# Five gather buffers, and a float32 activation in the fronts of a two-layer decoder step

## The chip, the core and the metric

The kernel runs on one core of a Trainium2 chip: TensorE (PE, with its weight loads as PEld), VectorE (DVE), ScalarE (ACT), GpSimd (POOL) and SyncE (SP) work side by side, each through its own instructions in a fixed order, and 16 DMA engines move data. The metric is the time of one execution in microseconds of the device; lower is better.

## The reference, cut to what matters

512 prompt tokens (four tiles of 128, numbered 0 to 3) and 8 sample tokens (tile 4) pass through two layers. Layer 0 is a gated MLP, layer 1 attention with shared keys and values; each is followed by the same expert block, which for each token picks 128 of 16384 experts:

```
q = (h @ w_q).reshape(T, 8, 2, 128)
s = einsum('thcd,hcnd->thcn', q, keys)        # 8 heads, 2 halves, 128 keys
sv, si = top_k(s, 16)                          # then the 16 best of the 256 sums per head
g = softmax(top_s)
u, vv = u_tab[eidx], v_tab[eidx]               # rows of 1024 numbers, 128 of each per token
act = gelu(einsum('thkd,td->thk', u, h))
out = einsum('thk,thkd->td', g * act, vv)
```

All numbers are float32.

## The kernel before, in words

**Two ways through the expert block.** In each layer two of the four tiles are done densely and two by gathering (`DT`: dense are tiles 0 and 1 in layer 0, tiles 2 and 3 in layer 1).

- *Gathered tiles* (`peer_tile`): for each of the 128 chosen experts GpSimd gathers one row of `peer_u` per token (`gather`, an indirect DMA of 512 KB into a tile of pool `gb`, tag `g`), and DVE multiplies it with `h_g` and sums it into a column of `act`. After 16 of them ScalarE applies the gelu, and 16 rows of `peer_v` are gathered and added to `x` by DVE. That makes 2 tiles x 256 = 512 gathers in each layer, 1024 in all, each with one DVE instruction over 128x1024 numbers. The pool has three buffers. A gather can be issued when the buffer that it takes has been read by DVE.
- *Dense tiles* (`dense_peer`): all 16384 experts are computed for 256 tokens, in four quarters of 32 blocks of 128 experts. `acts(q)` multiplies blocks of `peer_ut` (tile `ub`) with the activation, `gates(q)` builds the gates of the chosen experts by one-hot matrices and multiplies them in (`W`, L531), and the loop at the end multiplies `W` with blocks of `peer_v` (tile `vb`) into four PSUM banks `y`. The third and fourth quarters' `acts`, half of the second's, and the whole fourth quarter of `y`, are split products.

**Split products.** A float32 number is written as a sum of two float32r numbers, high and low; TensorE takes three float32r passes (high x high, high x low, low x high) in place of one float32 product. For a weight block `split` makes the high part on ScalarE (`wh`, L206) and the low part on DVE (`wl`, L208, one instruction of 128x1024). For the activation `norm_T` and `to_T` make the high part on ScalarE and the low part on DVE (`hTl`, L179 and L200).

**Fronts.** Before its expert block each layer has two groups of tiles (`GROUPS`): layer 0 first tile 2 alone, then tiles 0, 1, 3, 4; layer 1 first tile 0, then tiles 2, 3, 1, 4. `stage` counts these four fronts from 0. A front is the gated MLP or the attention, then `peer_front`: normalise, queries by `peer_wq` (16 weight blocks), scores against the keys, and the ranking on DVE (`topk_rank`, `topk_pick`). In the first front of a layer, which has one tile (and in layer 1 the sample's keys), products are float32. In the second, with up to 392 columns, `split_T` returns a float32r pair and `dense` splits each weight block; only `w_out` and `w_q` are float32 there. In the first quarter of `dense_peer` the pair is added up again into two float32 tiles `hF` (L538).

**What sets the order.** The program is traced once, and a scheduler with a model of the engines lays each engine's instructions in a fixed order. A list of anchors (`tick`) ties the n-th gather product of a layer to the n-th anchor, so that the gathers spread over the work beside them; this decides the place in the order and is no wait on the chip. Each engine then runs its order strictly: a DVE instruction that waits for a gather holds up all that stands behind it. Gathers of a layer start when the first front has chosen its tile's experts (`ix`, L671) and must be done before the next layer's front of those tiles.

**Buffers that the change touches.** Tag `h` (`HB[0]`: four of 128x1024 in layer 0, three in layer 1), tag `zT` (three), the activation `hT` in the permanent pool, `row4` for the sample tokens' rows of keys and queries, and a tile `cand` each for 8 heads and 1.

Of the kernel before, what the change touches and what calls it, by code (L numbers as in the profile page):

```python
# [18 lines left out]
D = 1024  # L19
S = 512  # L20
NB = 8
# [14 lines left out]
def body(ctx: ExitStack, tc: tile.TileContext, a):  # L36
# [4 lines left out]
    gb = ctx.enter_context(tc.tile_pool(name="gb", bufs=3))  # L41
# [35 lines left out]
    HB, NW = [4], [264]  # L77
# [105 lines left out]
    def split_T(name, both=False):  # L183

        if stage[0] == 2 or 1 and not stage[0]:
            return wa.tile([128, 8, 128], F32, name=name, tag="h", bufs=HB[0])
        pool, tag, n = (per, "hT", 392) if stage[0] else (wa, "hA", 256)
        if [0, 0, 0, 0][stage[0]] and not both:
            return pool.tile([128, 8, n], F32, name=name, tag=tag + "h", bufs=1)
        return [pool.tile([128, 8, n], FR, name=name + k, tag=tag + k, bufs=1) for k in "hl"]  # L190
# [20 lines left out]
    def dense(w, nk, rhs, n, consume, f0=0, f1=None, steps=None):  # L211

        f1 = w.shape[0] if f1 is None else f1
        for f in range(f0, f1):
            ps = pm.tile([128, 512], F32, name="ps_d", tag="mm")
            for c0 in range(0, nk, 8):
                wt = wp.tile([128, 8, 128], F32, name="wt", tag="wt")
                SY.dma_start(wt, w[f, :, c0:c0 + 8, :])
                if isinstance(rhs, list):
                    wh, wl = split(wt, [1, 2, 1, 2][stage[0]])  # L220
                    for c in range(8):
                        PE.matmul(ps[:, :n], wh[:, c, :], rhs[0][:, c, :n], start=c == 0, stop=False)  # L222
                        PE.matmul(ps[:, :n], wh[:, c, :], rhs[1][:, c, :n], start=False, stop=False)  # L223
                    for c in range(8):
                        PE.matmul(ps[:, :n], wl[:, c, :], rhs[0][:, c, :n], start=False, stop=c == 7)
                else:
                    for c in range(8):
                        z = PE.matmul(ps[:, :n], wt[:, c, :], rhs[:, c0 + c, :n], start=c0 + c == 0,  # L228
                                      stop=c0 + c == nk - 1)
                    tick(z, [6, 6, 6, 5][stage[0]])  # L230
            consume(f - f0, ps)
            step([4, 6, 4, 5][stage[0]] if steps is None else steps)

    def to_tok(n, tiles, func, tok):
        hold = {}

        def consume(ft, ps):
            q, i = divmod(ft, ZF)
            if i == 0:
                hold[0] = wa.tile([128, ZF, NW[0]], F32, name="zT", tag="zT", bufs=3)  # L240
# [23 lines left out]
    def gmlp(tiles, n, ph):  # L264
# [54 lines left out]
        def u_out(ft, ps):  # L319
            if ft % ZF == 0:  # L320
                hold[0] = wa.tile([128, ZF, NW[0]], F32, name="uT", tag="zT", bufs=3)
# [36 lines left out]
    def topk_rank(s, p, nh, state, h0):  # L358
# [14 lines left out]
        cand = wk.tile([128, nh, 88], F32, name="cand", tag=f"cand{nh}", bufs=1)[:p]  # L373
# [92 lines left out]
    def dense_peer(layer, dpa, open_rest, open_odd, smp):  # L466
        hT = dd["hT"]
        NQ, QI, NV = 4, 32, 4
# [4 lines left out]
        def acts(q):  # L473

            W[q] = (odd if q % 2 else dpa).tile([128, QI, 256], F32, name="W", tag="W", bufs=1)
            for il in range(QI):
# [3 lines left out]
                if (il * 5) % 32 < [[0, 16, 32, 32], [0, 16, 32, 32]][layer][q]:  # L480
                    uh, ul = split(u, [2, 3][layer] if q else [0, 1][layer])
                    for c in range(8):
                        PE.matmul(ps, uh[:, c, :], hT[0][:, c, :256], start=c == 0, stop=False)  # L483
                        PE.matmul(ps, uh[:, c, :], hT[1][:, c, :256], start=False, stop=False)  # L484
                    for c in range(8):
                        PE.matmul(ps, ul[:, c, :], hT[0][:, c, :256], start=False, stop=c == 7)  # L486
                else:
                    for c in range(8):
                        for k in range(2):
                            z = PE.matmul(ps[:, k * 128:(k + 1) * 128], u[:, c, :], hF[k][:, c, :], start=c == k == 0,  # L490
                                          stop=c == 7, skip_group_check=True)
                    tick(z, [2, 3][layer] if q else [0, 1][layer])
# [3 lines left out]
        def gates(q):  # L496
# [4 lines left out]
            for t0 in range(0, 256, 32):  # L501
# [32 lines left out]

        hF = [dpa.tile([128, 8, 128], F32, name=f"hF{k}", tag=['vb', 'vb'][k], bufs=3 if ['vb', 'vb'][k] == "vb" else 1)
              for k in range(2)]
        for k in range(2):
            V.tensor_tensor(hF[k], *[z.bitcast(F32)[:, :, k * 128:(k + 1) * 128] for z in hT], op=OP.add)  # L538
# [50 lines left out]
    def peer_front(tiles, n, layer, ph):  # L589
        if any(t == 4 or t not in DT[layer] for t in tiles):  # L590
            gbc = bcast_row(a["f_norm_g"][layer], D, f"g_f{layer}")
        hT = dd["hT"] = split_T("hT", True)
# [23 lines left out]
        if 4 in tiles:  # L616
            qz = [wa.tile([128, 8, 72], F32, name=f"qz{c}", tag="zT", bufs=3) for c in range(2)]
# [82 lines left out]
    def gather(table, ix, k, pool=None, tag="sg", nb=1):  # L700
        t = gb.tile([128, D], F32, name="gath", tag="g") if pool is None else \
            pool.tile([128, D], F32, name="gaths", tag=tag, bufs=nb)
# [64 lines left out]
    def run_layer(layer, setup):  # L767
# [11 lines left out]
        HB[0], NW[0] = 4 - layer, GROUPS[layer][1][1]  # L779
# [58 lines left out]
    def setup1(ph):  # L838
# [182 lines left out]
        def attn(tiles, n):  # L1021
# [6 lines left out]
            if first:  # L1028
                hT = per.tile([128, 8, 392], F32, name="hT", tag="hTh")
# [3 lines left out]
                row4 = per.tile([128, 2, D], F32, name="row4", tag="hTl")[:NB]  # L1033
                smp["v"] = ks.tile([128, D], F32, name="v_smp", tag="hs", bufs=1)[:NB]
                smp["kT"] = ph.tile([128, 8, NB], F32, name="kTs")
            else:
                hT = split_T("hT")
# [12 lines left out]
            def row(t, k):  # L1050
                return wa.tile([128, D], F32, name="kq_tok", tag="h", bufs=HB[0]) if t < 4 else row4[:, k]

            kt = {t: row(t, 0) for t in kqv}
# [9 lines left out]
            qt = {t: row(t, 1) for t in kqv}  # L1063
# [19 lines left out]
            oT = split_T("oT")  # L1083
# [120 lines left out]
```

## Time and profile before

| | |
|---|---|
| median of three runs | 3507.37 us (3499.5 to 3507.73) |
| the profiled execution | 3478.04 us, span 3476.3 us, granted TensorE clock 0.93 on the mean |
| busy: PE, PEld, DVE, ACT, POOL | 88%, 70%, 73%, 41%, 37% of the span |
| chain that ended last | PE 37%, DMA 27%, DVE 15%, issue 14%, POOL 6% |
| of it the gathers' DMAs | 15% `peer_v`, 9% `peer_u` |
| moved | 976.76 MB, on the mean 281 GB/s |

A busy share is the mean over stages with different limits, so it is read stage by stage. A wait is the idle time of an engine before an instruction and what ended it. In the chain, "issue" is time in which an engine waited for nothing that the profile shows.

### The profile page before, as it was taken

How to read it: one execution, taken by the hardware profiler on the slowest of the kernel's cores; microseconds unless marked ns; L12 is line 12 of the kernel's file. 1: busy time of each engine (PE TensorE's matmuls, PEld its weight loads, DVE VectorE, ACT ScalarE, POOL GpSimd, SP SyncE). 2: the span in 40 equal slices, each digit the busy share in tenths (PEclk: the TensorE clock that was granted, in tenths of full speed). 3: DMA queues.
4: the chain of work that ended last, by engine and by line, in shares of the span. 5: the costliest groups of instructions: out<-in, count | busy, mean ns of one | idle time of the engine just before them, and what ended most of it. 6: DMA issues, size and time to landing. Idle time of an engine off the chain costs nothing.

```text
span 3476.3 us, 53629 instructions
## 1 busy us (share of the span) xinstructions
PE 3063.4 (88%) x19776; PEld 2450.6 (70%) x19776; DVE 2545.1 (73%) x5191; ACT 1421.2 (41%) x3180; POOL 1289.9 (37%) x1061
## 2 busy tenths in 40 slices
PE   7988948779999999999888888646899999999998
PEld 7887538779757857757878643546899658758656
DVE  1478569888666777668657677779888666777778
ACT  2343022125565485664444344322236334343433
POOL 0034442334344344434320433442334444334343
PEclk9998979889999999999999988769899999999999
DMA  7677875778888989889985777775788889889888
GB/s 257 226 253 253 276 241 189 254 277 284 299 310 308 332 304 320 318 292 327 332 287 179 281 256 248 261 235 176 270 301 311 313 300 321 318 291 341 304 278 316
DMA packets 271576, 976.76 MB, mean 281 GB/s; under 512 B 30938, under 2 KB 31770, under 8 KB 271306
## 3 DMA queue, kind: packets, MB, share of 16 engines
q0 software_dynamic: 152064, 553.72, 46.5%
q1 hardware_dynamic: 119250, 419.62, 34.5%
q8 instruction: 155, 2.54, 0.3%
q14 instruction: 107, 0.88, 0.1%
HBM read 966.76 MB, written 6.46 MB: 280 GB/s over the span
## 4 chain that ended last, share of the span: by engine, by line
PE 37%; DMA 27%; DVE 15%; issue 14%; POOL 6%; ACT 1%; POOLq 0%; DVEq 0%; SPq 0%; ACTq 0%
DMA gath<-peer_v,ix 15%; PE y L573 10%; DMA gath<-peer_u,ix 9%; POOL gath L703 6%; PE ps_d L228 4%; DVE gath L712 3%; PE ps_g L528 3%; DVE x L719 3%; PE ps_a L486 3%; PE ps_a L490 3%; PE ps_a L483 3%; PE ps_a L484 3%; PE y L570 1%; DVE wl L208 1%; PE y L571 1%
## 5 line engine op out<-in xcount | busy, mean ns | idle before, releaser
L703 POOL DMA_INDIRECT gath<-peer_u,ix x512 | 634.2, 1239 | 1212.4 <-DVE gath L712 631.1
L703 POOL DMA_INDIRECT gath<-peer_v,ix x512 | 612.6, 1197 | 910.4 <-DVE x L719 531.4
L712 DVE SCALAR_TENSOR_TENSOR gath<-gath,h_g 128x1024 f32<-128x1024 f32 x512 | 622.9, 1222 | 298.0 <-DMA gath<-peer_u,ix 295.9
L719 DVE SCALAR_TENSOR_TENSOR x<-gath,act,x 128x1024 f32<-128x1024 f32 x512 | 656.2, 1282 | 246.1 <-DMA gath<-peer_v,ix 241.5
L573 PE MATMUL y<-vb,W 128*128 128x512 f32 x1536 | 718.6, 611 | 5.2 <-DVE W L531 5.2
L521 ACT ACTIVATE ohj<-iota,selJ 128x128 f16<-128x128 f32 x1408 | 423.8, 388 | 352.0 <-PE ps_g L528 351.7
L573 PEld LDWEIGHTS y<-vb,W 128*128 128x128 f32 x1536 | 285.4, 196 | 292.6 <-issue 287.2
L490 PE MATMUL ps_a<-hF,ub 128*128 128x128 f32 x3072 | 362.5, 281 | 50.9 <-DVE hF L538 50.3
L490 PEld LDWEIGHTS ps_a<-hF,ub 128*128 128x128 f32 x3072 | 358.6, 198 | 52.7 <-DVE hF L538 50.7
L528 PEld LDWEIGHTS <-ohj 128*128 128x128 f16 x4096 | 257.6, 130 | 94.1 <-issue 86.5
L483 PE MATMUL ps_a<-hTh,wh 128*128 128x256 f32 x1280 | 320.3, 288 | 0.0
L484 PE MATMUL ps_a<-hTl,wh 128*128 128x256 f32 x1280 | 312.4, 282 | 0.0
L528 PE MATMUL ps_g<-gi,ohj 128*128 128x32 f16 x4096 | 269.9, 233 | 11.6 <-DVE gaths L731 8.1
L206 ACT ACTIVATE wh<-ub 128x1024 fp32r<-128x1024 f32 x160 | 169.6, 1060 | 255.0 <-PE ps_a L484 205.0
L483 PEld LDWEIGHTS ps_a<-hTh,wh 128*128 128x128 f32 x1280 | 243.1, 190 | 3.4 <-issue 2.9
L484 PEld LDWEIGHTS ps_a<-hTl,wh 128*128 128x128 f32 x1280 | 242.7, 190 | 3.4 <-issue 3.4
L222 PE MATMUL ps_d<-hTh,wh 128*128 128x392 f32 (+1 forms) x640 | 230.7, 362 | 12.2 <-ACT qT L637 5.3
L223 PE MATMUL ps_d<-hTl,wh 128*128 128x392 f32 (+1 forms) x640 | 226.4, 355 | 3.5 <-DVE hTl L200 3.2
L208 DVE TENSOR_TENSOR wl<-ub,wh 128x1024 fp32r<-128x1024 f32 x160 | 194.9, 1222 | 43.2 <-ACT wh L206 37.8
L531 DVE TENSOR_TENSOR W<-ps_g,W 128x512 f32<-128x512 f32 x128 | 156.7, 1225 | 83.0 <-PE ps_g L528 82.5
L493 ACT ACTIVATE W<-ps_a 128x256 f32<-128x256 f32 x256 | 94.7, 374 | 275.1 <-PE ps_a L490 217.8
L206 ACT ACTIVATE wh<-wt 128x1024 fp32r<-128x1024 f32 x88 | 93.3, 1061 | 242.5 <-PE ps_d L223 168.3
(313 smaller groups left out, 4662.0 us busy)
## 6 DMA issues: line engine op xcount, KB each, us to landing
ub<-peer_ut SPq DMA_DIRECT2D x256, 512.0 KB, 5.2
vb<-peer_v SPq DMA_DIRECT2D x256, 512.0 KB, 5.3
wt<-w_in SPq DMA_DIRECT2D x64, 512.0 KB, 4.5
wt<-peer_wq SPq DMA_DIRECT2D x64, 512.0 KB, 4.3
wt<-w_out SPq DMA_DIRECT2D x32, 512.0 KB, 4.5
gath<-peer_u,ix POOLq DMA_INDIRECT x512, 6.1
gath<-peer_v,ix POOLq DMA_INDIRECT x512, 6.2
wt<-w_k SPq DMA_DIRECT2D x16, 512.0 KB, 5.6
```

The lines of the kernel that those rows point to most:

```text
L206: SC.activation(wh, w, AF.Copy)
L208: tick(V.tensor_tensor(wl, w, wh.bitcast(F32), op=OP.subtract), k)
L222: PE.matmul(ps[:, :n], wh[:, c, :], rhs[0][:, c, :n], start=c == 0, stop=False)
L483: PE.matmul(ps, uh[:, c, :], hT[0][:, c, :256], start=c == 0, stop=False)
L484: PE.matmul(ps, uh[:, c, :], hT[1][:, c, :256], start=False, stop=False)
L490: z = PE.matmul(ps[:, k * 128:(k + 1) * 128], u[:, c, :], hF[k][:, c, :], start=c == k == 0, stop=c == 7, skip_group_check=True)
L521: SC.activation(oh[:, :, k], iota128, AF.Abs, scale=-1.0, bias=selJ[:, t2 + k:t2 + k + 1])
L528: PE.matmul(ps[:, t - t1, :], oh[:, :, k], gi[:, c, :, t - t0], start=c == 0, stop=c == 1)
L573: PE.matmul(y[t][hf], w[:, ts], v[:, hs], start=i == 0, stop=i == 127)
L703: GP.indirect_dma_start(out=t, out_offset=None, in_=table, in_offset=bass.IndirectOffsetOnAxis(ap=ix[:, k:k + 1], axis=0))
L712: z = V.scalar_tensor_tensor(u, u, 1.0, h, op0=OP.mult, op1=OP.mult, accum_out=act[:, k:k + 1])
L719: z = V.scalar_tensor_tensor(x[t], v, act[:, k:k + 1], x[t], op0=OP.mult, op1=OP.add)
```

## The change

- The pool of the gathered rows has five buffers instead of three.
- The activation of a second front is one float32 tile (`full_T`), with float32 weight blocks, in `peer_front` of both layers and in the attention's key, value and output projections. Only the gated MLP of layer 0 (`split_T` at stage 1) keeps the pair.
- The expert phase makes its own pair `hP` from the float32 tile, with one ScalarE and one DVE instruction over 128x2048, while the first quarter runs. The first quarter multiplies the float32 tile directly, 256 columns at a time (before: twice 128 columns, from `hF`). The second quarter is split in all 32 blocks (before: in 16).
- Space: `hT` lies in pool `wk`, tag `h` has three buffers in both layers, tag `zT` two in layer 0, `cand` is shared, and the sample's rows of keys and queries come from tag `h`.
- The anchors of a float32 weight block in the last front are 3 instead of 5.

```diff
-    gb = ctx.enter_context(tc.tile_pool(name="gb", bufs=3))
+    gb = ctx.enter_context(tc.tile_pool(name="gb", bufs=5))
...
-    HB, NW = [4], [264]
+    HB, NW, ZB = [3], [264], [3]
...
-    def split_T(name, both=False):
-
-        if stage[0] == 2 or 1 and not stage[0]:
+    def full_T(name):
+
+        if stage[0] % 2 == 0:
             return wa.tile([128, 8, 128], F32, name=name, tag="h", bufs=HB[0])
-        pool, tag, n = (per, "hT", 392) if stage[0] else (wa, "hA", 256)
-        if [0, 0, 0, 0][stage[0]] and not both:
-            return pool.tile([128, 8, n], F32, name=name, tag=tag + "h", bufs=1)
-        return [pool.tile([128, 8, n], FR, name=name + k, tag=tag + k, bufs=1) for k in "hl"]
+        return wk.tile([128, 8, 392], F32, name=name, tag="hT", bufs=1)
+
+    def split_T(name):
+
+        if stage[0] != 1:
+            return full_T(name)
+        return [pool.tile([128, 8, 392], FR, name=name + k, tag="hT", bufs=1) for k, pool in (("h", wk), ("l", wa))]
...
-                    tick(z, [6, 6, 6, 5][stage[0]])
+                    tick(z, [6, 6, 6, 3][stage[0]])
...
         hT = dd["hT"]
+
+        hP = [dpa.tile([128, 8, 256], FR, name=f"hP{k}") for k in "hl"]
...
-                if (il * 5) % 32 < [[0, 16, 32, 32], [0, 16, 32, 32]][layer][q]:
-                    uh, ul = split(u, [2, 3][layer] if q else [0, 1][layer])
+                if q:
+                    uh, ul = split(u, [2, 3][layer])
                     for c in range(8):
-                        PE.matmul(ps, uh[:, c, :], hT[0][:, c, :256], start=c == 0, stop=False)
-                        PE.matmul(ps, uh[:, c, :], hT[1][:, c, :256], start=False, stop=False)
+                        PE.matmul(ps, uh[:, c, :], hP[0][:, c, :], start=c == 0, stop=False)
+                        PE.matmul(ps, uh[:, c, :], hP[1][:, c, :], start=False, stop=False)
                     for c in range(8):
-                        PE.matmul(ps, ul[:, c, :], hT[0][:, c, :256], start=False, stop=c == 7)
+                        PE.matmul(ps, ul[:, c, :], hP[0][:, c, :], start=False, stop=c == 7)
                 else:
                     for c in range(8):
-                        for k in range(2):
-                            z = PE.matmul(ps[:, k * 128:(k + 1) * 128], u[:, c, :], hF[k][:, c, :], start=c == k == 0,
-                                          stop=c == 7, skip_group_check=True)
-                    tick(z, [2, 3][layer] if q else [0, 1][layer])
+                        z = PE.matmul(ps, u[:, c, :], hT[:, c, :256], start=c == 0, stop=c == 7)
+                    tick(z, [0, 1][layer])
+                    if il == 1:
+                        SC.activation(hP[0], hT[:, :, :256], AF.Copy)
+                        V.tensor_tensor(hP[1], hT[:, :, :256], hP[0].bitcast(F32), op=OP.subtract)
...
-        for k in range(2):
-            V.tensor_tensor(hF[k], *[z.bitcast(F32)[:, :, k * 128:(k + 1) * 128] for z in hT], op=OP.add)
...
-        hT = dd["hT"] = split_T("hT", True)
+        hT = dd["hT"] = full_T("hT")
...
-        HB[0], NW[0] = 4 - layer, GROUPS[layer][1][1]
+        HB[0], NW[0], ZB[0] = 3, GROUPS[layer][1][1], 2 + layer
...
-                hT = split_T("hT")
+                hT = full_T("hT")
...
-            oT = split_T("oT")
+            oT = full_T("oT")
```

The scheduler lays out the whole program anew, so the change moves instructions far from these lines. Three places show how. The first is DVE's order at the start of `peer_front` in layer 0's second front, where `h_g`, `h_s` and `hTl` belong to the normalised activation and `gath` to tile 2's gathers. Before:

```order
L712 SCALAR_TENSOR_TENSOR gath,act<-gath,h_g 128x1024 x2
L606 SCALAR_TENSOR_TENSOR h_s_3140<-xs_t,r,g_f_3039 8x1024
L179 SCALAR_TENSOR_TENSOR hTl<-ps_t,gcols,hTh 128x128 x2
L712 SCALAR_TENSOR_TENSOR gath,act<-gath,h_g 128x1024
L179 SCALAR_TENSOR_TENSOR hTl<-ps_t,gcols,hTh 128x128 x2
L712 SCALAR_TENSOR_TENSOR gath,act<-gath,h_g 128x1024
L612 TENSOR_TENSOR h_s<-h_s_3140,h_s 8x1024
L179 SCALAR_TENSOR_TENSOR hTl<-ps_t,gcols,hTh 128x128 x3
```

The same place after the change:

```order
L713 SCALAR_TENSOR_TENSOR gath,act<-gath,h_g 128x1024 x2
L607 SCALAR_TENSOR_TENSOR h_s_3121<-xs_t,r,g_f_3039 8x1024
L713 SCALAR_TENSOR_TENSOR gath,act<-gath,h_g 128x1024 x2
L613 TENSOR_TENSOR h_s<-h_s_3121,h_s 8x1024
L717 TENSOR_TENSOR act<-act,gate 128x16
L720 SCALAR_TENSOR_TENSOR x_70<-gath,act,x_70 128x1024 x14
L655 COPY qz_3154<-qT 128x2x8
L720 SCALAR_TENSOR_TENSOR x_70<-gath,act,x_70 128x1024 x2
```

The low halves are gone, and 16 gather products that stood between weight splits and rankings now stand in two runs ahead of the ranking of this front. The second place is DVE's order in the fourth quarter of layer 0's expert phase, where each of 28 `vb` blocks needs one `wdl` and one `wl`. Before:

```order
L564 TENSOR_TENSOR wdl<-W,wdh 128x256
L208 TENSOR_TENSOR wl<-vb,wh 128x1024
L719 SCALAR_TENSOR_TENSOR x_80<-gath,act,x_80 128x1024
L564 TENSOR_TENSOR wdl<-W,wdh 128x256
L208 TENSOR_TENSOR wl<-vb,wh 128x1024
L719 SCALAR_TENSOR_TENSOR x_80<-gath,act,x_80 128x1024
```

The same place after the change:

```order
L565 TENSOR_TENSOR wdl<-W,wdh 128x256 x3
L211 TENSOR_TENSOR wl<-vb,wh 128x1024
L565 TENSOR_TENSOR wdl<-W,wdh 128x256
L211 TENSOR_TENSOR wl<-vb,wh 128x1024
L565 TENSOR_TENSOR wdl<-W,wdh 128x256
L211 TENSOR_TENSOR wl<-vb,wh 128x1024
```

Layer 0's gathers have ended by then; before, 75 of them stood behind the last gate product (L531) of layer 0, the last 42 of these in layer 1's first front. The third place is PE's order where `peer_front` of layer 0 ends and the first quarter's `acts` begin (`ps_s` and `ps_ss` are scores). Before:

```order
L646 MATMUL ps_s<-keysT,qT 128x128 x3
L657 MATMUL ps_ss_3179<-keysT,qz_3175 64x128 x2
L646 MATMUL ps_s<-keysT,qT 128x128 x9
L657 MATMUL ps_ss_3180<-keysT,qz_3176 64x128 x2
L490 MATMUL ps_a<-hF_3903,ub 128x128 x4
```

The same place after the change:

```order
L231 MATMUL ps_d<-hT,wt 128x392 x32
L494 MATMUL ps_a<-hT,ub 128x256 x3
L647 MATMUL ps_s<-keysT,qT 128x128 x3
L658 MATMUL ps_ss_3158<-keysT,qz_3154 64x128 x2
L494 MATMUL ps_a<-hT,ub 128x256 x3
L647 MATMUL ps_s<-keysT,qT 128x128 x5
```

The first quarter reads `hT`, which the front has written, and no longer `hF`, which DVE had to add up; its first blocks stand among the last scores.

## Rows read from the trace of the kernel before

**Rows 1.** Windows: busy us (instructions) of each engine by stretch, then clock, DMA.
```profile
196.00:475.00 279.00, 225.14 (x1055) 183.14 (x1053) 186.22 (x274) 65.56 (x110) 127.14 (x103) 0.90 0.81 273
475.00:783.00 308.00, 229.18 (x1636) 222.89 (x1637) 267.80 (x962) 78.33 (x149) 105.55 (x85) 0.85 0.69 236
783.00:1666.00 883.00, 859.47 (x5733) 636.58 (x5731) 643.67 (x797) 527.58 (x1246) 371.25 (x301) 0.98 0.88 310
1666.00:1899.00 233.00, 200.15 (x1494) 188.16 (x1495) 145.62 (x477) 106.71 (x289) 46.00 (x40) 0.92 0.75 262
1899.00:2268.00 369.00, 288.09 (x1164) 191.84 (x1162) 274.58 (x537) 132.69 (x276) 155.41 (x132) 0.83 0.78 260
2268.00:2545.00 277.00, 188.45 (x1264) 179.17 (x1265) 243.24 (x902) 66.16 (x118) 100.19 (x86) 0.84 0.70 234
2545.00:3476.00 931.00, 903.02 (x6100) 682.22 (x6098) 709.56 (x912) 376.94 (x837) 383.03 (x312) 0.98 0.88 309
```

**Rows 2.** DVE's waits, 196 to 475 us: total us, times, longest.
```profile
DVE gath L712 <- DMA gath<-peer_u,ix: 50.4, 30, 4.0
DVE x L719 <- DMA gath<-peer_v,ix: 38.4, 29, 3.9
```

**Rows 3.** DVE's waits, 475 to 783 us.
```profile
DVE gath L712 <- DMA gath<-peer_u,ix: 16.9, 13, 2.2
DVE x L719 <- DMA gath<-peer_v,ix: 15.3, 14, 3.6
```

**Rows 4.** DVE's waits, 1899 to 2268 us.
```profile
DVE gath L712 <- DMA gath<-peer_u,ix: 37.8, 32, 3.8
DVE x L719 <- DMA gath<-peer_v,ix: 31.0, 24, 2.9
```

**Rows 5.** DVE's waits, 2268 to 2545 us.
```profile
DVE x L719 <- DMA gath<-peer_v,ix: 17.5, 13, 3.2
DVE gath L712 <- DMA gath<-peer_u,ix: 14.7, 13, 3.9
```

**Rows 6.** PE's waits, 475 to 783 us.
```profile
PE ps_a L490 <- DVE hF L538: 25.6, 1, 25.6
PE ps_t L172 <- ACT xr L168: 24.8, 1, 24.8
PE ps_t L196 <- DVE hTl L179: 13.1, 2, 12.3
```

**Rows 7.** The gathers' tile: count, ns min/median/max, first and last start.
```profile
L703 POOL DMA_INDIRECT gath<-peer_u,ix x512: 932/940/5075, 196.5 to 3411.9; - x171
...
L719 DVE SCALAR_TENSOR_TENSOR x<-gath,act,x x512: 1215/1284/1467, 242.9 to 3471.1; 128x1024 f32<-128x1024 f32 x171
...
DMA to landing us min/median/max: 4.1/6.1/9.9
```

**Rows 8.** Groups by line, shapes apart: count | busy us, mean ns | idle before.
```profile
L208 DVE TENSOR_TENSOR wl<-wt,wh 128x1024 fp32r<-128x1024 f32 x88 | 107.5, 1221 | 11.6 <-ACT wh L206 5.6 <-ACT kq_tok L1044 3.5 <-ACT uv L276 2.2
L179 DVE SCALAR_TENSOR_TENSOR hTl<-ps_t,gcols,hTh 128x128 fp32r<-128x128 f32 x80 | 24.6, 342 | 14.7 <-ACT hTh L178 14.3
```

**Rows 9.** PE's timeline, second front of layer 0: start, us, instruction.
```profile
345.28 1.50 PE L305 MATMUL ps_mix<-wsT_m,uv 128*128 128x128 f32 x12
356.53 21.23 PE L228 MATMUL ps_d<-uv,wt 128*128 128x392 f32 x64
```

**Rows 10.** PE's timeline, first gates of layer 0.
```profile
836.16 1.98 PE L528 MATMUL ps_g<-gi,ohj 128*128 128x32 f16 x32
843.73 2.16 PE L528 MATMUL ps_g<-gi,ohj 128*128 128x32 f16 x32
...
852.95 1.98 PE L528 MATMUL ps_g<-gi,ohj 128*128 128x32 f16 x32
```

**Rows 11.** PE's timeline, fourth quarter of layer 0.
```profile
1600.52 1.09 PE L569 MATMUL y<-wh,wdh 128*128 128x512 f32 x4
1603.32 1.09 PE L569 MATMUL y<-wh,wdh 128*128 128x512 f32 x4
```

More of the change, by code (lines that the diff above doesn't have):

```diff
@@ L239, in consume @@
             if i == 0:
-                hold[0] = wa.tile([128, ZF, NW[0]], F32, name="zT", tag="zT", bufs=3)
+                hold[0] = wa.tile([128, ZF, NW[0]], F32, name="zT", tag="zT", bufs=ZB[0])
             z = hold[0]
@@ L320, in u_out @@
             if ft % ZF == 0:
-                hold[0] = wa.tile([128, ZF, NW[0]], F32, name="uT", tag="zT", bufs=3)
+                hold[0] = wa.tile([128, ZF, NW[0]], F32, name="uT", tag="zT", bufs=ZB[0])
             u = hold[0]
@@ L372, in topk_rank @@
                 yield
-        cand = wk.tile([128, nh, 88], F32, name="cand", tag=f"cand{nh}", bufs=1)[:p]
+        cand = wk.tile([128, nh, 88], F32, name="cand", tag="cand", bufs=1)[:p]
         def add(o, a0, na, nb):
@@ L532, in gates @@
                     yield
-        hF = [dpa.tile([128, 8, 128], F32, name=f"hF{k}", tag=['vb', 'vb'][k], bufs=3 if ['vb', 'vb'][k] == "vb" else 1)
-              for k in range(2)]
-        for k in range(2):
-            V.tensor_tensor(hF[k], *[z.bitcast(F32)[:, :, k * 128:(k + 1) * 128] for z in hT], op=OP.add)
         for _ in acts(0):
@@ L616, in peer_front @@
         if 4 in tiles:
-            qz = [wa.tile([128, 8, 72], F32, name=f"qz{c}", tag="zT", bufs=3) for c in range(2)]
+            qz = [wa.tile([128, 8, 72], F32, name=f"qz{c}", tag="zT", bufs=ZB[0]) for c in range(2)]
             for z in qz:
@@ L698, in sample_finish, with gather @@
         yield
-    def gather(table, ix, k, pool=None, tag="sg", nb=1):
+    def gather(table, ix, k, pool=None):
         t = gb.tile([128, D], F32, name="gath", tag="g") if pool is None else \
-            pool.tile([128, D], F32, name="gaths", tag=tag, bufs=nb)
+            pool.tile([128, D], F32, name="gaths", tag="sg", bufs=1)
         GP.indirect_dma_start(out=t, out_offset=None, in_=table,
@@ L1028, in attn @@
             if first:
-                hT = per.tile([128, 8, 392], F32, name="hT", tag="hTh")
+                hT = wk.tile([128, 8, 392], F32, name="hT", tag="hT", bufs=1)
                 zb = hT[:, :, nq:nq + 256]
@@ L1032, in attn @@
                 hT = hT[:, :, :nq]
-                row4 = per.tile([128, 2, D], F32, name="row4", tag="hTl")[:NB]
                 smp["v"] = ks.tile([128, D], F32, name="v_smp", tag="hs", bufs=1)[:NB]
@@ L1048, in heads, with row @@
                 return [(dst[t][:rows[t]].rearrange("p (h d) -> p h d", d=64), rows[t]) for t in kqv]
-            def row(t, k):
-                return wa.tile([128, D], F32, name="kq_tok", tag="h", bufs=HB[0]) if t < 4 else row4[:, k]
-            kt = {t: row(t, 0) for t in kqv}
+            def row(t):
+                return wa.tile([128, D], F32, name="kq_tok", tag="h", bufs=HB[0])[:rows[t]]
+            kt = {t: row(t) for t in kqv}
             dense_tok(a["w_k"], 8, hT, nq, kqv, AF.Copy, rows_out(kt))
@@ L1062, in attn @@
                     to_T(kt[t], NB, smp["kT"], 0)
-            qt = {t: row(t, 1) for t in kqv}
+            qt = {t: row(t) for t in kqv}
             dense_tok(a["w_q"], 8, hB, nq, kqv, AF.Copy, rows_out(qt))
```

## The prediction

> **What bounds the kernel now.** I read the busy time of every engine stretch by stretch first, since the whole-run shares (PE 88%, DVE 73%) hide that the limit changes [rows 1]. Between 783 and 1666 us and between 2545 and 3476 us, the two expert phases, PE is busy 859 of 883 and 903 of 931 us: there only PE's own work counts. In the other stretches PE is busy 63 to 86%. For those I then read what DVE waited for. From 196 to 475 us DVE works 186 us and waits 50.4 + 38.4 = 89 us for gathers [rows 2]: together 275 of 279. From 475 to 783 it is 268 + 32 = 300 of 308 [rows 3], from 1899 to 2268 it is 275 + 69 = 344 of 369 [rows 4], from 2268 to 2545 it is 243 + 32 = 275 of 277 [rows 5]. So in the fronts DVE's row of work sets the end, and its only large wait is the gathers. What PE waits for there (one xr, the low halves hTl, the sum hF: 25.6 + 24.8 + 13.1 us [rows 6]) comes late out of DVE's row.
>
> Why DVE waits is seen in the gathers' own tile [rows 7]: a gather is issued in 0.94 us, lands after a median of 6.1 us, and its product takes 1.28 us, after which the buffer is free. One buffer's round is 6.1 + 0.94 + 1.28 = 8.32 us; three buffers give one gather per 2.77 us. From 196 to 475 us DVE had 100 gathers in its order: 275 / 100 = 2.75 us each. That stretch runs at the three buffers' pace.
>
> **The change part by part.** The profiled execution took 3478.04 us; the median of the runs is 3507.37, 1.0084 times that. I sum against the profiled time and multiply at the end. Counts per stretch are taken from the two orders of DVE, cut at the same landmarks (last mix of the front, first gate product, and so on). Gathers, before to after: 100 to 104, 84 to 125, 286 to 283, 42 to 0, 131 to 164, 83 to 71, 297 to 277; the second column makes 1024, the first 1023 (one falls on a border).
>
> *Five buffers.* The pace allowed by buffers becomes 8.32 / 5 = 1.66 us per gather. Another limit takes over: from 196 to 475 us the DMA engines moved 279 x 273 = 76 MB at a share of 0.81, so at full share this takes 226 us, with four more gathers (2 MB) 232; PE's work there is 225 us. The bounds for that stretch are thus 279 (nothing gained) and 232. I take the middle, **-25 us**: it leaves DVE with 254 - 186 - 5 = 63 us of waits on 104 gathers in place of 89 on 100, two thirds (0.65 per gather is used below). Both ends stay in the range.
>
> *475 to 783 us (the rest of layer 0's second front).* 41 more gathers x 1.28 = +52. The 16 peer_wq splits go, 1.22 us each [rows 8]: -20. Sixteen low halves of 0.34 us and their small fellows: -7. The waits, 32 us on 84 gathers, become 32 x 125/84 x 0.65 = 31. DVE: 268 + 25 + 31 = 324 in place of 300, +24. The 25.6 us that PE waits for hF is DVE's row too and does not come off by itself; that the first quarter reads hT and its first blocks stand among the last scores lets PE start earlier, for which I take off a quarter of it: **+18**. PE's cost here: a float32 block of 392 columns takes 21.23 / 4 = 5.31 us, two split ones with two mixes of up to 1.50 us 356.53 - 345.28 = 11.25, so some 4.2 each, the mixes overlapping a little [rows 9]; 16 blocks x about 1.0 = 16 on top of 229 of 308 us, hidden by DVE's row.
>
> *Expert phase of layer 0.* In the second quarter all 32 blocks are split, 16 more. Two split blocks and a gate take 843.73 - 836.16 = 7.57 us, two float32 ones and a gate 852.95 - 843.73 = 9.22 [rows 10]: 0.83 us a block, -13. DVE gets 16 splits, 20 us, and has 883 - 644 = 239 idle, but they fall early, where the run of late gathers also stands; half of it, +10. The tail's pace is PE's: 12 products per block in 1603.32 - 1600.52 = 2.80 us [rows 11], so the gathers that leave it give no pace back, only part of the 24 us of PE idleness: -12. Sum **-15**.
>
> *1666 to 1899 us (layer 1's first front).* All 42 gathers leave DVE, 54 us of work. But PE works 200 of 233 us there [rows 1]; of the 33 idle I take half: **-15**.
>
> *1899 to 2268 us (ranking, second front's attention).* 33 more gathers, +42; 24 splits of w_k, w_v, w_o gone, -29; waits 69 x 164/131 x 0.65 = 56 in place of 69. DVE: 275 + 13 + 56 = 344, as before. PE gets 24 x 1.0 = 24, to 312 of 369. But the extra gathers stand in the attention, the removed splits elsewhere; part of one doesn't pay for the other: **+10**.
>
> *2268 to 2545 us.* 12 gathers fewer, -15; 16 splits, -20; low halves, -5; waits 32 x 71/83 x 0.65 = 18, -14: -54. PE rises to 188 + 16 = 204, far below. I take 70%, since rankings wait for scores too: **-38**.
>
> *Expert phase of layer 1.* As in layer 0: -13 for the second quarter, and of 28 us of PE idleness -12: **-25**.
>
> *Without effect:* hP costs one ScalarE copy and one DVE subtraction of 128x2048, hF's two sums of 128x1024 go, the same 2.4 us of DVE; ScalarE is busy 528 of 883 us in the phase. The first quarter's 256 columns at once cost PE as many columns as twice 128. HB three in place of four, ZB two, cand shared and row4 in tag h take spare buffers away; no wait for them stands among the large ones before [rows 6]; a new one is bounded by the largest PE wait there, 25.6 us, and by nothing, and I take nothing. The tick of 3 acts only through the order, counted above. Before 196 us no gather runs: 0.
>
> Sum: -25 + 18 - 15 - 15 + 10 - 38 - 25 = **-90**, 3388 us profiled, x 1.0084 = **3417 us**.
>
> **The rivals.** *Waits vanish.* If five buffers give DVE every gather in time, the remaining waits fall out: another 22 us in the first stretch down to its floor of 232, some 20, 30 and 10 in the later ones: -170 in all, 3308, **3336**. For it: 1.66 us is well under what DVE uses per gather with its other work. Against: a DMA share of 0.81 already there.
>
> *Issue sets the pace.* If POOL's issue of the next gather only starts when DVE's product ends, a gather in a run takes 1.28 + 0.94 = 2.22 us, however many buffers there are. Runs of six and more gathers with nothing between them hold 161 in the new order, 60 in the old. 101 x 0.94 = 95 us; half of it on the path is +47: -43, 3435, **3464**. For it: issues that took up to 5.08 us at a median of 0.94 [rows 7]. Against: they overlap products now, and DVE's product stays at 1.22 to 1.47.
>
> The Trainium skill ("SBUF — State Buffer", Who interferes with whom) says that a DVE instruction with two SBUF inputs contends with a GpSimd instruction that reads SBUF, and that one of them then blocks fully. By that rule this rival would hold and the sum come to 3464; the trace bears it out in the issues' long tail, not in their median.
>
> *The transfers bind, buffers give nothing.* The waits per gather stay, factor 1 in place of 0.65: 5 + 35 - 15 - 15 + 30 - 32 - 25 = -17, 3461, **3490**; 7 us more on the path make it no change. For it: all stretches with gathers move 234 to 310 GB/s, and five gathers in flight may each land later than 6.1 us.
>
> *Bursts hold up the row (slower).* DVE is strictly in order. In the new order 16 gathers stand ahead of layer 0's ranking, 14 ahead of the fourth quarter's splits in layer 1. If each of the 101 further gathers in runs makes DVE stand 1.5 us (three buffers' pace, 2.77 - 1.28) and what is behind them is what PE needs, this adds 152 us: -90 + 152 = +62, 3540, **3570**. It decides from 90 / 101 = 0.9 us of standing, that is from 2.2 us per gather in a run. Against: five buffers fill before a run, and 1.66 is below 2.2.
>
> **How the numbers follow.** Forecast 0.42, waits vanish 0.21, issue 0.13, transfers bind 0.13, bursts 0.11. The forecast's own range is 3380 to 3455 (first stretch and the waits' factor at their ends). The range 3335 to 3500 leaves out the bursts and the outer halves of two rivals. A measurement tells 0.3%, 10.5 us, from no change: forecast, vanish, issue and a third of "transfers bind" are faster, 0.80; the rest of that one is split, same 0.06, with slower 0.14 with the bursts.
>
> **What would show it.** In the changed profile: DVE's waits for gathers in the four stretches near 63 + 31 + 56 + 18 = 168 us (222 before); landing longer than 6.1; the stretch to the end of layer 0's gated MLP at about 254 us; the one to the first gates longer than 308; layer 1's first front free of gather products, about 218; its scores' stretch about 240; the second quarter at 7.57 us per two blocks. Wrong it would be if these waits stay above 200 us, if landing rises towards 10 us, or if PE waits on W or on wdl behind runs of gathers in the expert phases.

## The result

The changed kernel takes **3341.3 us** (median of 4 runs, 3338.09 to 3345.37) against 3507.55 us before: a ratio of **0.953**, 95% interval 0.9511 to 0.9549. That is faster and inside the range of 3335 to 3500, but 76 us below the forecast of 3417 and below the forecast's own range of 3380 to 3455.

The profiled execution took 3338.09 us with a span of 3336.4. The page of the changed kernel, its busy shares and the chain that ended last:

```profile
PE 3075.3 (92%) x18048; PEld 2313.2 (69%) x18048; DVE 2493.2 (75%) x5093; ACT 1380.6 (41%) x3154; POOL 1379.0 (41%) x1061
...
PE 66%; DVE 12%; DMA 9%; issue 6%; POOL 3%; ACT 3%; another core or an unknown queue 0%; SPq 0%; DVEq 0%; POOLq 0%; ACTq 0%
PE y L574 19%; PE ps_d L231 8%; PE ps_g L534 7%; PE ps_a L488 6%; PE ps_a L489 5%; PE ps_a L491 5%; PE ps_a L494 3%; POOL gath L704 3%; DMA gath<-peer_u,ix 3%; DMA gath<-peer_v,ix 3%; DVE x L720 2%; DVE gath L713 2%; PE y L570 2%; PE y L571 2%; PE y L572 2%
```

The two gather DMAs are 3% each of the chain, where they were 9% and 15%, and PE has gone from 37% to 66%. The windows of the changed kernel, cut at the same landmarks as those of before [rows 1], with the same columns (PE, PEld, DVE, ACT, POOL, granted clock, DMA share, GB/s):

```profile
196.00:428.00 232.00, 217.60 (x1054) 179.22 (x1052) 187.34 (x280) 63.90 (x108) 150.62 (x109) 0.97 0.92 335
428.00:749.00 321.00, 243.94 (x1038) 185.21 (x1039) 294.26 (x987) 65.42 (x140) 165.37 (x126) 0.86 0.84 297
749.00:1625.00 876.00, 855.14 (x5568) 631.39 (x5565) 655.92 (x804) 535.21 (x1256) 386.04 (x295) 0.97 0.86 310
1625.00:1825.00 200.00, 181.57 (x1418) 167.45 (x1417) 82.60 (x388) 90.13 (x275) 0.00 (x0) 0.97 0.57 185
1825.00:2182.00 357.00, 311.56 (x1044) 170.21 (x1043) 289.07 (x559) 114.87 (x262) 212.77 (x169) 0.86 0.90 325
2182.00:2415.00 233.00, 193.80 (x780) 139.54 (x778) 207.29 (x846) 51.18 (x104) 86.04 (x71) 0.93 0.73 257
2415.00:3336.00 921.00, 902.01 (x5819) 674.04 (x5817) 702.11 (x899) 392.94 (x854) 376.83 (x289) 0.97 0.84 298
```

Set beside the prediction, stretch by stretch (us):

| stretch | before | predicted | measured |
|---|---|---|---|
| first gathers to the end of the gated MLP | 279 | 254 | 232 |
| to layer 0's first gate product | 308 | 326 | 321 |
| expert phase of layer 0 | 883 | 868 | 876 |
| layer 1's first front | 233 | 218 | 200 |
| ranking, second front's attention | 369 | 379 | 357 |
| rest of that front | 277 | 239 | 233 |
| expert phase of layer 1 | 931 | 906 | 921 |
| sum of changes | | -90 | -140 |

The fronts together lost 123 us (predicted 50), the expert phases 17 (predicted 40). DVE's waits for gathers in the changed kernel, two rows for each of the four stretches of [rows 2 to 5], in their order in time:

```profile
DVE gath L713 <- DMA gath<-peer_u,ix: 24.7, 26, 3.8
DVE x L720 <- DMA gath<-peer_v,ix: 10.6, 14, 1.6
...
DVE x L720 <- DMA gath<-peer_v,ix: 10.3, 9, 2.8
DVE gath L713 <- DMA gath<-peer_u,ix: 8.6, 7, 2.2
...
DVE gath L713 <- DMA gath<-peer_u,ix: 28.8, 25, 7.1
DVE x L720 <- DMA gath<-peer_v,ix: 11.5, 11, 4.6
...
DVE gath L713 <- DMA gath<-peer_u,ix: 12.2, 9, 4.8
DVE x L720 <- DMA gath<-peer_v,ix: 2.0, 3, 0.8
```

They add up to 109 us: 222 before, 168 predicted. The first stretch took the 232 us that had been named as its floor, but not for the reason named: the DMA engines stood at a share of 0.92 and not at 1, and at 335 GB/s. DVE's work and its waits for gathers, 187 + 35 us, and PE's 217.6 us of work each nearly fill the stretch.

### The profile page after: what moved, and what is told of

It is laid out like the page before. It is cut to its first block, busy times and chain, and to the rows that moved or that the text cites. A ratio compares the mean times of both kernels' runs of the same rounds, so it can differ in the third digit from the quotient of the medians.

```text
span 3336.4 us, 50069 instructions
## 1 busy us (share of the span) xinstructions
PE 3075.3 (92%) x18048; PEld 2313.2 (69%) x18048; DVE 2493.2 (75%) x5093; ACT 1380.6 (41%) x3154; POOL 1379.0 (41%) x1061
## 4 chain that ended last, share of the span: by engine, by line
PE 66%; DVE 12%; DMA 9%; issue 6%; POOL 3%; ACT 3%; another core or an unknown queue 0%; SPq 0%; DVEq 0%; POOLq 0%; ACTq 0%
PE y L574 19%; PE ps_d L231 8%; PE ps_g L534 7%; PE ps_a L488 6%; PE ps_a L489 5%; PE ps_a L491 5%; PE ps_a L494 3%; POOL gath L704 3%; DMA gath<-peer_u,ix 3%; DMA gath<-peer_v,ix 3%; DVE x L720 2%; DVE gath L713 2%; PE y L570 2%; PE y L571 2%; PE y L572 2%
## 5 line engine op out<-in xcount | busy, mean ns | idle before, releaser
L704 POOL DMA_INDIRECT gath<-peer_u,ix x512 | 679.5, 1327 | 1096.3 <-DVE ix L672 488.8
L704 POOL DMA_INDIRECT gath<-peer_v,ix x512 | 660.0, 1289 | 708.4 <-DVE x L720 381.1
L231 PE MATMUL ps_d<-hT,wt 128*128 128x128 f32 (+3 forms) x2048 | 428.2, 367 | 26.9 <-DMA wt<-peer_wq 8.2
L488 PE MATMUL ps_a<-hPh,wh 128*128 128x256 f32 x1536 | 404.8, 300 | 11.2 <-ACT wh L209 11.2
L231 PEld LDWEIGHTS ps_d<-hT,wt 128*128 128x128 f32 x2048 | 302.6, 198 | 138.3 <-issue 17.5
L489 PE MATMUL ps_a<-hPl,wh 128*128 128x256 f32 x1536 | 385.6, 287 | 0.0
L488 PEld LDWEIGHTS ps_a<-hPh,wh 128*128 128x128 f32 x1536 | 301.0, 196 | 25.5 <-ACT wh L209 13.3
L489 PEld LDWEIGHTS ps_a<-hPl,wh 128*128 128x128 f32 x1536 | 300.8, 196 | 10.3 <-issue 10.3
L494 PE MATMUL ps_a<-hT,ub 128*128 128x256 f32 x1024 | 233.3, 390 | 27.7 <-ACT W L499 27.7
L494 PEld LDWEIGHTS ps_a<-hT,ub 128*128 128x128 f32 x1024 | 199.6, 196 | 58.0 <-ACT W L499 28.5
L491 PE MATMUL ps_a<-hPh,wl 128*128 128x256 f32 x1536 | 226.7, 291 | 1.8 <-DVE wl L211 1.8
```

What stands on the lines that cost most here:

```text
L488: PE.matmul(ps, uh[:, c, :], hP[0][:, c, :], start=c == 0, stop=False)
L489: PE.matmul(ps, uh[:, c, :], hP[1][:, c, :], start=False, stop=False)
L491: PE.matmul(ps, ul[:, c, :], hP[0][:, c, :], start=False, stop=c == 7)
L494: z = PE.matmul(ps, u[:, c, :], hT[:, c, :256], start=c == 0, stop=c == 7)
L704: GP.indirect_dma_start(out=t, out_offset=None, in_=table, in_offset=bass.IndirectOffsetOnAxis(ap=ix[:, k:k + 1], axis=0))
```

## The experiments

The question was which part made the gain: the buffers (theory A), or the relief of DVE by the float32 activation (theory B). Each kernel was compared with the kernel before on its own chip, and a ratio below is its time over that kernel's. The scheduler lays out the instructions of each kernel anew, so the places of the gathers differ too. Not run was the other half of the question, the kernel before with five buffers and nothing else.

**Three buffers, the rest as changed.**

```diff
-    gb = ctx.enter_context(tc.tile_pool(name="gb", bufs=5))
+    gb = ctx.enter_context(tc.tile_pool(name="gb", bufs=3))
```

> The changed kernel with three gather buffers in place of five, nothing else. Theory A, the buffers are the gain: DVE's waits for gathers in the four stretches of the fronts come back from 109 to over 200 us, the stretch from the first gather to the end of layer 0's gated MLP is 275 to 280 us again in place of 232, and the time is 3430 to 3480 us. Theory B, the float32 activation is the gain (DVE is rid of 40 splits and 66 low halves in the fronts, and the buffers only hide what would be hidden anyway): 3340 to 3380 us, waits below 150 us.

Measured: 3506.89 us, ratio to the kernel before 1.0002 (0.9988 to 1.0016). Theory B is dead: without the two extra buffers all the other edits together give nothing. The time is also 27 us above theory A's figures, which had left the other edits a gain. (The splits that leave the fronts are 56, 88 before and 32 after, and not 40.) The windows of this kernel for the six stretches up to the last expert phase, and DVE's two largest waits in the whole run:

```profile
197.00:482.00 285.00, 225.18 (x1054) 182.22 (x1052) 184.39 (x273) 63.72 (x108) 129.72 (x104) 0.89 0.79 266
482.00:802.00 320.00, 239.27 (x1008) 182.22 (x1009) 273.09 (x961) 64.23 (x137) 122.85 (x107) 0.86 0.77 264
802.00:1675.00 873.00, 854.47 (x5593) 632.72 (x5592) 642.06 (x784) 540.89 (x1258) 363.61 (x288) 0.97 0.86 305
1675.00:1887.00 212.00, 186.03 (x1422) 171.19 (x1421) 122.66 (x440) 94.06 (x278) 31.51 (x31) 0.94 0.74 259
1887.00:2289.00 402.00, 316.36 (x1045) 172.81 (x1044) 271.20 (x541) 110.89 (x260) 169.45 (x152) 0.85 0.80 267
2289.00:2558.00 269.00, 201.57 (x784) 144.16 (x785) 226.35 (x865) 51.37 (x104) 101.75 (x86) 0.87 0.75 252
```

```profile
DVE gath L713 <- DMA gath<-peer_u,ix: 304.1, 218, 6.8
DVE x L720 <- DMA gath<-peer_v,ix: 245.3, 191, 4.7
```

The first stretch is back at 285 us. The other edits do move time, but nearly cancel: against [rows 1], -10 in layer 0's expert phase, -21 in layer 1's first front and -8 in the rest of its second, +6 in the first stretch, and +12 and +33 in the two where 105 and 149 gathers stand in DVE's order (84 and 131 before), with three buffers to serve them. DVE's waits for gathers over the whole run are 549 us, 537 before and 150 in the changed kernel. The attention, the fifth row, runs at the pace of the ring: with this kernel's median landing of 5.9 us, (5.9 + 0.94 + 1.28) / 3 = 2.71 us per gather, and the stretch has 402 / 149 = 2.70.

**Four buffers.** The same line with `bufs=4`.

> The changed kernel with four gather buffers. By the round of one buffer (6.1 + 0.94 + 1.28 = 8.32 us) four give a gather per 2.08 us, 104 of them 216 us, which is under the 232 us that the DMA engines need in the first stretch. Theory A: nearly all of the gain is there, 3350 to 3380 us, first stretch 235 to 250 us. Rival, the gain grows with every buffer, because landings get longer with more in flight: midway between three and five, 3390 to 3410 us, first stretch near 255 us.

Measured: 3367.26 us, ratio 0.9607 (0.9576 to 0.9638): 140 of the 166 us are there with one buffer more. Window of the first stretch of this kernel:

```profile
196.00:447.00 251.00, 219.78 (x1053) 179.71 (x1051) 185.56 (x277) 63.27 (x108) 139.09 (x107) 0.94 0.88 308
```

251 us is just over what theory A expected and near the rival's 255, while the whole time is theory A's: one buffer gives most, the second some. From the gathers' tile of this kernel, the time from a gather's issue to its landing:

```profile
DMA to landing us min/median/max: 4.1/6.5/10.6
```

A landing is 6.5 us here and 6.1 before [rows 7], so the rival's mechanism is real: (6.5 + 0.94 + 1.28) / 4 = 2.18 us per gather, 5% over the 2.08 expected. For 104 gathers that is 227 us, so the round does not explain the 251 us of the whole stretch. It does explain the runs, in which six or more gather products follow each other in DVE's order with nothing between them. Over all such runs of a trace, the mean time from one product to the next, beside the round over the buffers:

| buffers | round / buffers | measured in runs |
|---|---|---|
| three, the kernel before | 2.77 | 2.49 |
| three, the rest as changed | 2.71 | 2.62 |
| four | 2.18 | 2.13 |
| five, the changed kernel | 1.82 | 1.83 |

(The landing for five buffers, 6.9 us, is that of the next kernel.) So the ring sets the pace inside the runs with five buffers too; what a buffer changes is how fast a run goes by. A run of 16 in the changed kernel, its first and last product, 28.35 us apart:

```profile
1832.69 1.23 DVE L713 SCALAR_TENSOR_TENSOR gath<-gath,h_g 128x1024 f32<-128x1024 f32 x1 [7.08 <-DMA gath<-peer_u,ix]
...
1861.04 1.23 DVE L713 SCALAR_TENSOR_TENSOR gath<-gath,h_g 128x1024 f32<-128x1024 f32 x1 [1.34 <-DMA gath<-peer_u,ix]
```

**DVE's splits put back, unused.** The `peer_wq` blocks of both second fronts are split again, but the products stay float32 and read nothing of it.

```diff
                 else:
+                    if dummy:
+                        split(wt, 0)
...
-            dense(a["peer_wq"][layer], 8, hT, n, q_out, sp * 4, sp * 4 + 4, [5, 2, 4, 3][stage[0]])
+            dense(a["peer_wq"][layer], 8, hT, n, q_out, sp * 4, sp * 4 + 4, [5, 2, 4, 3][stage[0]],
+                  stage[0] % 2 == 1)
```

> The changed kernel, in which the peer_wq blocks of the second fronts (16 in each layer) are split again by ScalarE and DVE, but the halves are not used and the products stay float32: DVE gets 2 x 16 x 1.22 = 39 us of work back. Theory A (DVE's row still sets the end of these stretches): 3370 to 3385 us, both stretches longer by 15 to 20 us. Rival (with five buffers something else ends them, PE or the scores): under 3355 us.

Measured: 3376.79 us, ratio 0.9616 (0.96 to 0.9632), 35 us more than the changed kernel's 3341.3, for 39 us of DVE's work; by the ratios, with 0.953 for the changed kernel above or the 0.9562 of a later measurement, it is 30 or 19 us. The windows of this kernel for the two stretches that got the splits, and its gathers' landing:

```profile
431.00:765.00 334.00, 243.98 (x1051) 185.88 (x1051) 311.73 (x1004) 81.61 (x158) 170.38 (x127) 0.85 0.80 286
2217.00:2475.00 258.00, 199.90 (x787) 143.15 (x788) 225.26 (x864) 65.30 (x118) 88.05 (x73) 0.89 0.68 235
```

```profile
DMA to landing us min/median/max: 4.1/6.9/12.8
```

They grew by 13 and 25 us; two executions of the changed kernel differ there by 0 and 2 us. In the first, DVE's work and its waits for gathers fill 312 + 21 of 334 us, so DVE's row still sets the end. In the second, 8.7 us are DVE's waits for ScalarE's high halves, which came back with the splits. The two together are 38 us for 39 us of work: with five buffers an instruction removed from DVE's row is worth nearly its duration, while with three the same removal, and more, gave nothing. So the two parts of the change are no plain sum. Against a clean price stands that the attention, which got no splits, took 375 us here in place of 357, for a reason that stays open.

**Second quarter half in float32.** 16 of its 32 blocks are single products again. They take the high half of the activation as their operand and leave out the low one. (With `hT` itself as the operand the kernel deadlocks, so it has no time.)

```diff
-                if q:
+                if (il * 5) % 32 < [0, 16, 32, 32][q]:
...
-                        z = PE.matmul(ps, u[:, c, :], hT[:, c, :256], start=c == 0, stop=c == 7)
-                    tick(z, [0, 1][layer])
+                        z = PE.matmul(ps, u[:, c, :], (hP[0].bitcast(F32) if q else hT)[:, c, :256],
+                                      start=c == 0, stop=c == 7)
+                    tick(z, [2, 3][layer] if q else [0, 1][layer])
```

> The changed kernel with 16 of the second quarter's 32 blocks as float32 products in place of three passes; they take the high half of the activation alone as their float32 operand, so these 16 blocks leave out its low half. By the prediction's term (0.83 us of PE per block, 16 blocks, two layers) the time is 3341 + 27 = 3368 us. Rival, DVE's 16 splits a layer held up what stands behind them and cost as much as PE gained: 3335 to 3345 us.

Measured: 3352.32 us, ratio 0.955 (0.9511 to 0.9588); the interval holds the changed kernel's 0.953. So the extra splits are worth some 7 us (0.002 x 3507), not 27, and not surely more than nothing; against the later 0.9562 the sign turns. Windows from layer 0's first to its 16th gate product, where 28 of the second quarter's blocks are multiplied: first the changed kernel, then this one.

```profile
749.00:877.00 128.00, 118.83 (x1144) 114.03 (x1142) 123.53 (x152) 89.58 (x203) 72.76 (x46) 0.96 0.86 302
```

```profile
751.00:873.00 122.00, 122.00 (x1036) 112.42 (x1034) 105.55 (x137) 74.98 (x187) 61.90 (x46) 1.00 0.87 317
```

With all blocks split, 28 in place of 14, PE's work is only 3 us less, where the term gives 14 x 0.83 = 12, and the granted clock is 0.96 in place of 1.00. The stretch is 6 us longer: DVE is busy for 123.5 of 128 us there, and PE waits. The waits of the changed kernel's PE from 749 to 1625 us say for what:

```profile
PE ps_a L488 <- ACT wh L209: 9.0, 4, 4.0
PE ps_g L534 <- ACT ohj L530: 7.3, 4, 2.2
```

The first row falls in that window: ScalarE's high halves come late, and ScalarE itself waits there 7.6 us for PE and 5.4 us for DVE's low halves. In layer 1 the splits do pay: from the first gate product to the end of the phase it takes 869 us with all blocks split and 878 with half of them, where layer 0 takes 876 and 873.

**Gathers moved by the anchors.** In the changed kernel DVE's order has 125 gathers in the stretch before layer 0's first gate product, which DVE ends, and none in the fourth quarter's tail, the stretch from the last gate product to the end of the phase. The anchors of a float32 block decide that.

```diff
-                    tick(z, [6, 6, 6, 3][stage[0]])
+                    tick(z, [6, 4, 6, 3][stage[0]])
```

> The changed kernel with 4 anchors in place of 6 per float32 weight block in layer 0's second front. In DVE's order 45 gathers leave the stretch from the end of the gated MLP to the first gate product (125 to 80) and 45 stand in the fourth quarter's tail, where there were none. Theory A, DVE's row ends that stretch: it loses up to 45 x 1.28 = 58 us, PE's 244 us of work becomes its floor, so 321 to about 275 us; the tail gives some 10 to 15 back: 3305 to 3320 us. Rival, scores and rankings end the stretch, and the tail suffers: 3335 to 3350 us.

Measured: 3339.17 us, ratio 0.9505 (0.9471 to 0.9539): not told apart from the changed kernel, and 20 us above what was expected. Windows of that stretch and of layer 0's tail in this kernel, and of the tail in the changed one:

```profile
432.00:714.00 282.00, 234.73 (x1002) 178.32 (x1003) 243.44 (x919) 64.35 (x137) 112.59 (x82) 0.92 0.74 259
1506.00:1616.00 110.00, 98.91 (x400) 76.55 (x400) 102.36 (x129) 45.05 (x69) 60.63 (x43) 0.94 0.95 353
...
1530.00:1625.00 95.00, 93.28 (x399) 74.83 (x396) 53.57 (x67) 42.25 (x63) 0.00 (x0) 0.96 0.55 169
```

The stretch lost 39 us, nearly the 46 of theory A, but the tail grew from 95 to 110, with DVE busy for 102.4 and the DMA engines at 0.95 of their time, and the rest of the expert phase by another 11, from 781 to 792. Two executions of the changed kernel differ by 7 us in that rest, so the 11 are not sure. With `[6, 6, 6, 2]` instead, the same was tried in layer 1:

> The changed kernel with 2 anchors in place of 3 per float32 weight block in layer 1's second front: 28 gathers leave the attention (164 to 136), 18 the stretch behind it (71 to 53), and 53 in place of 15 stand in the last quarter's tail. Theory A: the two stretches lose together 35 to 45 us, the tail gets 38 x 1.28 = 49 us of DVE and gives 20 back, 3315 to 3325 us. Rival, at the end of the program nothing lies behind the tail and it gives all back: 3341 to 3360 us.

Measured: 3346.03 us, ratio 0.9547 (0.9511 to 0.9582): the rival, nothing gained. Both together, `[6, 4, 6, 2]`:

> Both anchors changed, 4 in layer 0's second front and 2 in layer 1's. The two act in different layers: if each gain is one of a stretch of its own, they add, so the ratio to the changed kernel is the product of those of the two runs with one of them (3290 to 3305 us by theory A). Rival, the later gathers of layer 0 delay layer 1's front, and the sum is missed by more than 10 us.

Measured: 3332.36 us, ratio 0.9498 (0.9469 to 0.9528), 27 us above the upper end of theory A's figures. By the product of the two single effects it would be 0.952 of the kernel before, 8 us more: the two do not hinder each other. But the intervals are too wide for gains this small, so three kernels were timed more often, side by side on one chip: the changed one,

> The changed kernel once more, as the yardstick of the two beside it on the same chip: 0.953 of the kernel before, 3341 us or up to 0.3% more.

the last one again,

> Again 4 anchors in layer 0's second front and 2 in layer 1's, beside the changed kernel on one chip. If moving gathers out of the stretches that DVE ends pays at all, 10 to 15 us less than the changed kernel; if the tails and layer 1 give everything back, within 5 us of it.

and one with `[6, 5, 6, 2]`, which puts 14 gathers into layer 0's tail in place of 45:

> 5 anchors in layer 0's second front and 2 in layer 1's: 14 gathers stand in layer 0's tail in place of 45 (and of none in the changed kernel), 112 in place of 125 in the stretch before the first gate product. If the tail gives back only what exceeds DVE's idle time there (94 - 53 = 41 us, 32 products), the 14 are free and this is the fastest of the three, 3320 to 3328 us; if every gather moved is worth the same, it lies between the other two.

Measured, on that chip: 3348.76 (3343.17 to 3356.38, ratio 0.9562, 0.9536 to 0.9588), 3338.38 (3332.2 to 3343.11, ratio 0.9531) and **3336.14 us** (3333.49 to 3339.49, ratio 0.9527). The last two are faster than the changed kernel, by 10 and 13 us (no run of theirs is as long as its shortest), and not told apart from each other. Windows for the same stretch and tail, first of the last kernel, then of the changed one on this chip:

```profile
433.00:741.00 308.00, 236.81 (x990) 179.33 (x991) 278.22 (x968) 64.24 (x137) 142.91 (x114) 0.87 0.82 292
1531.00:1625.00 94.00, 92.73 (x392) 74.46 (x392) 68.67 (x81) 42.21 (x64) 14.70 (x10) 0.97 0.68 231
...
435.00:756.00 321.00, 242.62 (x1045) 184.59 (x1046) 294.80 (x988) 66.35 (x142) 162.38 (x126) 0.86 0.83 296
1544.00:1638.00 94.00, 92.28 (x388) 74.02 (x388) 52.96 (x66) 42.07 (x62) 0.00 (x0) 0.96 0.51 169
```

The 14 gathers are free: DVE's work in the tail rose from 53.0 to 68.7 us and the tail is 94 us in both. The stretch before the first gate product lost 13 us against its 321. With 45 in the tail DVE and the DMA engines are both near their limit; which of the two sets its length was not separated. The expected 3320 to 3328 were counted from 3341; from its yardstick on this chip, 3348.76, the 13 us are the low end of that gain.

## Why the prediction held, and where it was off

**Mechanism: right.** DVE's row, with its waits for gathers, set the end of the fronts; five buffers take half of the waits there away. The kernel with three buffers shows it, and the runs show that their pace follows the round of one buffer over the number of buffers. What the buffers give alone is not shown; with 39 us of DVE's relief undone (the splits put back) the rest still gave 130 us.

**The number: only the wide range held.** 3341 lies outside the forecast's own range, and inside the stated one only because that reached down to a rival. Of the 76 us, 50 are the stretches (-140 for -90), and 25 are the factor from the profiled time to the median.

**Factor 0.65 for the remaining waits: mis-sized.** It came from the middle between 279 and 232 us for the first stretch; the stretch took 232. That this was the floor was partly luck: the 232 came from a DMA share of 1 at the rate of before (273 GB/s at 0.81), while 335 GB/s at 0.92 would allow 213 us for the same bytes, as an estimate. Waits per gather fell from 0.89 to 0.34 us there (35.3 on 104), to 0.15, 0.25 and 0.20 in the other three: 0.4 to 0.5 of before. With 59 us of waits this is the largest error.

**Layer 1's first front: mis-sized,** -33 for -15. All gathers left, as said; but PE's busy 200 us was taken for fixed, and it fell to 181.6 (with 1418 records for 1494), while the granted clock rose from 0.92 to 0.97. With three buffers, and 31 gathers issued in it, the stretch was already 21 us shorter, so most of this is not the buffers' doing. In the first stretch PE's work likewise fell from 225 to 218 us as the clock rose from 0.90 to 0.97.

**Attention: wrong in sign,** -12 for +10. DVE's work rose to 289 us, as worked out (288), and PE's to 312 (312), but the waits fell to 40 us and not to 56. The stretch took 357 to 375 us in four kernels whose orders have the same 164 gathers in it, though both executions of the changed kernel took 357; why stays open.

**Rest of the two second fronts: right,** +13 for +18 and -44 for -38; the splits put back show that DVE's row sets the first, and that it counts in the second. hP cost no wait of PE. The waits for hF, 25.6 us in layer 0 and 24.7 in layer 1, are gone, but half of them came back in another place: ScalarE writes the first quarter's `W` only when DVE has finished a ranking (`si`), and PE waits for that. In layer 0 and in layer 1:

```profile
ACT W L499 <- DVE si L369: 21.8, 1, 21.8
PE ps_a L494 <- ACT W L499: 12.1, 1, 12.1
...
ACT W L499 <- DVE si L369: 17.6, 1, 17.6
PE ps_a L494 <- ACT W L499: 15.6, 1, 15.6
```

The prediction had taken nothing for new waits of this kind.

**Second quarter: mis-sized.** 0.83 us per block, read where splits and float32 blocks alternate, holds only while DVE and ScalarE keep up. With all blocks split they don't in layer 0, where 28 blocks and their gates took 128 us, 9.1 for two in place of 7.57, with 12 products of `y` among them. The expert phases gave 7 and 10 us in place of 15 and 25; the sum for layer 1 had also left out the 10 us for DVE that the one for layer 0 has.

**Profiled time to median: wrong step.** Before, the profiled execution was 0.8% under the median of the timed runs; after, 0.1% (3338.09 and 3341.3). The factor 1.0084 on the right profiled time would have given 3366, 25 us too many. One execution of the kernel before takes 3478 to 3525 us over all runs here, the profiled one being the shortest, so the factor was the scatter of one execution and nothing that a change carries over.

**A small misreading:** PE's least busy stretch among the fronts was at 188 of 277 us, 68% and not 63%; nothing was worked out from it.

**The rivals.** "Waits vanish" gave 3336 us and so nearly the time, but by luck: its stretches sum to -170 where -140 were measured, 109 us of waits are left in the fronts, and the factor 1.0084 made up the difference. "Transfers bind": landings do get longer with the buffers, 5.9, 6.5 and 6.9 us for three, four and five (6.9 in the kernel with the splits put back, which has five; the changed kernel's own trace does not tell it), but two more landings in flight outweigh that. "Issue": the rows of the page show mean issues of 1327 and 1289 ns where they were 1239 and 1197:

```profile
L704 POOL DMA_INDIRECT gath<-peer_u,ix x512 | 679.5, 1327 | 1096.3 <-DVE ix L672 488.8
L704 POOL DMA_INDIRECT gath<-peer_v,ix x512 | 660.0, 1289 | 708.4 <-DVE x L720 381.1
```

The median of the `peer_u` issues rose too, from 0.94 to 1.14 us. But in the runs a gather takes 1.83 us, where this rival needed 2.22 however many buffers there are, and the runs get faster with each buffer: the issue is not what sets their pace. The Trainium skill ("SBUF — State Buffer", Who interferes with whom) says that a DVE instruction with two SBUF inputs contends with a GpSimd instruction that reads SBUF; if the issue of a gather, which reads `ix`, counts as one, the longer issues agree in direction, but no run here separates this from other causes. "Bursts": in the two crowded stretches, with 125 and 164 gathers, DVE waited 0.15 and 0.25 us per gather, where this rival needed 0.9, and 1.83 us per gather in a run is below its 2.2. With three buffers it is real: those two stretches are 12 and 33 us longer than before.

## What to carry to other kernels

Where an in-order engine consumes transfers through a ring of buffers, work out the round of one buffer (landing, issue, use) over their number and compare it with the pace seen: 8.32 / 3 = 2.77 against 2.75 us told that three buffers were the limit. It is the pace inside runs of uses, and that of a whole stretch only where the ring is the limit throughout: here the fourth buffer brought 140 of the 166 us and the fifth the rest. While such waits set the pace, freeing the consumer of other work gave nothing here; afterwards 39 us of it were worth 38 in the stretches it stood in. A factor between one profiled execution and a median of others should not be carried over to the changed kernel.

## What was not expected of the hardware

The mean granted TensorE clock rose where PE's idle time shrank: from 0.90 to 0.97 in the first stretch (54 us idle before, 14 after), from 0.92 to 0.97 in layer 1's first front (33 and 18), from 0.84 to 0.93 in the rest of its second (89 and 39). PE's own work became shorter with it: in the first stretch the same products took 217.6 us in place of 225.1. And the gathers and weight loads together moved 335 GB/s in the first stretch, where they moved 273 before; the DMA share rose only from 0.81 to 0.92, so a share of 1 would be 337 GB/s by the first and 364 by the second: it is no fixed rate.
